# Sums of squares from a second, token-major load of x, and an earlier fetch of the output weights, in one encoder layer

## The chip, the cores and the metric

The kernel runs on one core of a Trainium2 chip, in float32. The measure is device time in microseconds of one execution, lower is better. A core has five engines that run their own instruction streams and wait for each other by semaphores: PE (TensorE, the matmuls; its loading of weights is listed apart as PEld), DVE (VectorE), ACT (ScalarE), POOL (GpSimd) and SP (SyncE, which here only issues transfers). Matmul results land in PSUM, everything else lives in SBUF.

## What is computed

One layer of an encoder on 1024 tokens of width 1024. The parts that matter here:

```python
h = rms_norm(x, norm1_g)                 # x * rsqrt(mean(x*x over the width) + eps) * gain
proj = h @ w_in                          # q, k, v (512 wide each) and u (512 wide)
a = neighbourhood_attention(rms_norm(q), rms_norm(k), v, rpb)   # 8 heads x 64
p = multiscale_pool(u, w_pool, pool_scale)
x = x + concat(a, p) @ w_out             # the output projection and its residual
h2 = rms_norm(x, norm2_g)
x = x + (silu(h2 @ w_gate) * (h2 @ w_up)) @ w_down
```

## The kernel before

Every operand of a matmul is split into a high part and a low part (`split`: ACT casts, DVE subtracts), and each product is three matmuls: high by high, high by low, low by high. `x` lies in HBM in two layouts. `xT` has the width on the 128 partitions, in 8 chunks `k` of 128x1024; `xt` has the tokens on the partitions, in 8 tiles `t` of 128x1024. All loads go through `fetch` (line 120), which takes one of 45 equal SBUF buffers and issues the transfer on SP's queue. SP works off its row in order, with at most eight transfers under way.

**Start.** SP fetches `xT` chunk by chunk, with the first weights `w1` in between, then `wp` and the first `wu` (the weights of the pooling branch). For each chunk `cook_x_` (line 170) lets ACT write `xh`, the high part of gain times `x`, DVE write `xl`, the low part, ACT write the squares `xsq`, and POOL add these up in `acc`; the last addition is shared by POOL and DVE. The first projection runs over `k`, and for each `k` over the token tiles `t` (8 for the first two chunks, 6 for the others), into PSUM banks `pj`. Its matmuls do not wait for the norm: `1/rms` comes in later, when a bank is read. At `k == KSS == 6` sixteen matmul instructions with a column of ones turn `acc` into the sums per token in a corner of a `pj` bank (`ss_ps`); from it come `vx`, `evx` and `rstd` (`rsqrt`: a logarithm and an exponential on ACT, then three Newton steps on DVE). After the last chunk TensorE does 18 matmuls for tile 6, then the first transposes `qkt` (`turn(0)`). These read `qn`, the normalised q and k that `pair(0)` makes on ACT and DVE once `rstd` is there.

**Middle.** Attention goes in steps named by head pair, column block and row block (2_3_1 is pair 2, block 3, row block 1). One step's scores `s` are transposed two steps later (`pt`), and multiplied with the values three steps later (`po`); in between lie the exponential on ACT, a scaling on POOL, and `split` into `pt_h` (ACT) and `pt_l` (DVE). Between the steps a generator, `g_dense` (line 802), feeds TensorE with dense work: projections, then the output projection `w_out` in two column halves. The output weights `wo_c_h` (chunk pair `c`, half `h`) come through `fetch_wo` and are split by `cook_wo`. At pair 3, `proj_shift` sends eight transfers on SP's queue that shift the values across partitions (`vsh`, `vsl`).

**End.** The last products of the down projection add into four quarters `c` of the output. `down` fills a PSUM bank, `dadd` adds it to the result on DVE, and `ship` sends it out.

A scheduler sets the order of most instructions before the program runs; those marked by `keep`, `keepd` and `pin` stay in the order in which they are written. On each engine the order is then fixed, and an instruction that waits holds up all behind it.

Of the kernel before, what the change touches and what calls it, by code (L numbers as in the profile page):

```python
# [54 lines left out]
def hybrid_block(ctx, tc, xT, xt, w1, wu, rpbx, wpool, wout, wgu, wd, g2, sm, out):  # L55
# [112 lines left out]
    acc = None  # L168

    def cook_x_(k):  # L170
        nonlocal acc
        raw = raws.pop(("x", k))
        h = slot(F32R, f"xh_{k}")
        l = slot(F32R, f"xl_{k}")
        n = 512 if k == 0 else T
        for c in range(0, T, n):
            cs = slice(c, c + n)
            keep(nc.scalar.activation(h[:, cs], raw[:, cs], AF.Copy, scale=g1_sb[:, k : k + 1]))  # L178
            nc.vector.scalar_tensor_tensor(  # L179
                out=l[:, cs],  # L180
                in0=raw[:, cs],
                scalar=g1_sb[:, k : k + 1],
                in1=h[:, cs].bitcast(F32),
                op0=ALU.mult,
                op1=ALU.subtract,
            )
            yield
        sq = slot(F32, f"xsq_{k}")
        nc.scalar.activation(sq, raw, AF.Square)
        if k:  # L190
            m = 512 if k == KC - 1 else 0
            nc.gpsimd.tensor_tensor(out=acc[:, m:], in0=acc[:, m:], in1=sq[:, m:], op=ALU.add)
            if m:
                nc.vector.tensor_tensor(out=acc[:, :m], in0=acc[:, :m], in1=sq[:, :m], op=ALU.add)
        else:
            acc = sq
        xh.append(h)
        xl.append(l)
# [267 lines left out]
    for i in range(4):  # L466
        if i:
            fetch_w1(0, i)
            fetch(("x", 2 * i), xT[2 * i], [P, T])
        fetch(("x", 2 * i + 1), xT[2 * i + 1], [P, T])  # L470
        if i == 3:
            fetch(("wp",), wpool, [P, 4, P])
    fetch_wu(0)
    pin_act = True
    for i in range(4):
# [8 lines left out]
        cook_x(2 * i + 1)  # L484
    pin_act = False
    one1 = up.tile([P, 1], F32, name="one1", bufs=1)
    nc.gpsimd.memset(one1, 1.0)
# [5 lines left out]
    ss_ps = pj[0][:, 384 : 384 + NT]  # L493
    for k in range(KC):
        ts = range(8 if k < KE else 6)
        for h in ((0, 1, 2),) if k > 1 else ((0, 1), (2,)) if k else ((0,), (1,), (2,)):
            for t in ts:
                if k == KSS:
                    for s in (t,) if t < 4 else (2 * t - 4, 2 * t - 3):
                        mm(  # L500
                            ss_ps[:, s : s + 1],
                            acc[:, s * P : s * P + P],
                            one1,
                            start=False,
                            stop=True,
                            skip_group_check=True,
                        )
                for i in h:
                    proj_pass(0, t, pj[t], k, i)
        if k == KSS:  # L510
            nc.vector.tensor_scalar(
                out=vx, in0=ss_ps, scalar1=1.0 / DM, scalar2=EPS, op0=ALU.mult, op1=ALU.add
# [289 lines left out]
    def g_dense():  # L802
# [4 lines left out]
        x2.extend(slot(F32, f"x2_{t}") for t in range(NT))  # L807
        for t in range(4):
            nc.sync.dma_start(out=x2[t], in_=xt[t])
        yield "wo"  # L810
        gs = [w_out(t, 0, six, 0) for t in range(3)]
# [6 lines left out]
        for c2 in (2, 3):  # L818
            fetch_wo(c2, 1)
# [8 lines left out]
        for t in range(4):  # L828
            for i, _ in enumerate(w_out(t, 1, six, 0)):
                if i % 3 == 2 and t < 3:  # L830
                    split_mix(six[2 * t + i // 3], 1, nc.scalar, (nc.gpsimd, nc.vector)[i // 3])
                yield
            nc.sync.dma_start(out=x2[4 + t], in_=xt[4 + t])
# [457 lines left out]
    for n in range(len(works)):  # L1291
# [5 lines left out]
        if not chain:  # L1297
            banks = [bank(pool[c], f"p{'aabccdd'[k]}_{g}_{c}") for c in range(4)]
        for c in range(4):
            ps = banks[c]  # L1300
            step_ = 256 if last and k == 6 and c == 3 else 512
            for n0 in range(0, 512, step_):
                n1 = n0 + step_
                down(g, ps[:, n0:n1], c, o, bo, chain, n0, n1)
# [86 lines left out]
```

## Time and profile before

| | |
|---|---|
| three timed runs | 1032.41 us median (1028.47 to 1033.79) |
| profiled execution | 1032.75 us, of which the span of instructions 1031.0 us |
| PE busy | 1010.6 us, 98% of the span |
| DVE / ACT / POOL busy | 64% / 41% / 41% |
| chain that ended last | PE 91%, DVE 4%, issue 2%, ACT 2%, DMA 1% |
| HBM | 86.25 MB read, 28.57 MB written |

PE counts as busy while a matmul is in the array, at full or at half clock. The time that PE could give back is therefore in two places: where it is idle, and where its granted clock (1.0 is 2.4 GHz) is below one. Both are found by stage, in the busy time by stretches, and then instruction by instruction in the timeline. In the timeline the bracket at the end of a row is the idle time of the engine in front of the instruction and what ended it.

### The profile page before, as it was taken

What the parts mean: (1) busy time and instruction counts of PE and PEld (TensorE: products, weight loads), DVE (VectorE), ACT (ScalarE), POOL (GpSimd) and SP (SyncE); (2) the same over time, 40 slices, a digit from 0 to 9 for tenths busy, and PEclk for the clock granted to TensorE, in tenths of its full rate; (3) what the DMA queues carried; (4) which work ended last, traced back from release to release, by engine and by line L of the source; (5) the groups of instructions that cost most, each with busy time, mean ns of one, the idle gap of its engine ahead of it and who ended that gap; (6) DMA issues with size and microseconds to landing.
All of it is one profiled execution on the core that took longest, in us unless ns stands there. A gap on an engine that the chain in (4) does not pass through costs nothing.

```text
span 1031.0 us, 13679 instructions
## 1 busy us (share of the span) xinstructions
PE 1010.6 (98%) x4909; PEld 869.1 (84%) x4909; DVE 662.5 (64%) x1115; ACT 426.8 (41%) x868; POOL 419.9 (41%) x456
## 2 busy tenths in 40 slices
PE   8899999999899998999999999999999999999998
PEld 7888999999788887888888888888888888888887
DVE  7767766667663568765655455455552499988872
ACT  8233566666762336522332333333231354533410
POOL 7210324244461146376559558558644400000170
PEclk9999999999999999999999999999999999999999
DMA  8100513143620323114233233233126984373402
GB/s 296 55 29 1 126 49 108 35 125 109 201 80 22 124 101 113 52 63 143 110 125 113 72 122 113 72 123 113 72 82 214 345 275 153 107 243 121 125 31 93
DMA packets 48821, 119.93 MB, mean 116 GB/s; under 512 B 5168, under 2 KB 13872, under 8 KB 48752
## 3 DMA queue, kind: packets, MB, share of 16 engines
q1 hardware_dynamic: 41824, 94.65, 28.2%
q0 software_dynamic: 5632, 20.19, 5.2%
q10 hardware_dynamic: 1296, 4.20, 1.0%
q8 instruction: 39, 0.64, 0.3%
q14 instruction: 30, 0.25, 0.1%
HBM read 86.25 MB, written 28.57 MB: 111 GB/s over the span
## 4 chain that ended last, share of the span: by engine, by line
PE 91%; DVE 4%; issue 2%; ACT 2%; DMA 1%; SPq 0%; ACTq 0%; DVEq 0%
PE w L89 12%; PE z L89 12%; PE pj L89 11%; PE x L89 11%; PE pw L89 7%; PE pd L89 6%; PE y L89 6%; PE pc L89 6%; PE pa L89 6%; PE pu L89 4%; PE pb L89 3%; PE s L89 2%; PE po L89 2%; PE pt L94 1%; DVE xl L179 1%
## 5 line engine op out<-in xcount | busy, mean ns | idle before, releaser
L89 PE MATMUL x<-b_h,w 128*128 128x512 f32 x352 | 115.8, 391 | 0.0
L89 PE MATMUL pw<-wo,mx 128*128 128x512 f32 x384 | 94.4, 397 | 0.5 <-DVE vnl L291 0.3
L89 PE MATMUL pj<-w1h,xl 128*128 128x384 f32 x256 | 85.0, 341 | 4.3 <-DVE xl L179 4.3
L89 PE MATMUL pj<-w1h,xh 128*128 128x384 f32 x256 | 88.4, 349 | 0.4 <-ACT xh L178 0.4
L89 PE MATMUL pj<-w1l,xh 128*128 128x384 f32 x256 | 86.0, 340 | 0.0
L1317 POOL TENSOR_TENSOR x2r<-x2r,u 128x512 f32<-128x512 f32 x12 | 23.8, 2020 | 149.8 <-DVE u L1277 149.8
L89 PEld LDWEIGHTS pw<-wo,mx 128*128 128x128 f32 x384 | 70.9, 189 | 14.8 <-DVE vnl L291 0.7
L89 PEld LDWEIGHTS x<-b_h,w 128*128 128x128 f32 x352 | 66.0, 188 | 13.6
L615 POOL TENSOR_SCALAR e<-e,r 128x256 f32<-128x256 f32 (+1 forms) x64 | 36.9, 577 | 82.2 <-DVE r L614 81.9
L1038 POOL TENSOR_TENSOR ur<-ur,gr 128x512 f32<-128x512 f32 x33 | 52.9, 1604 | 40.2 <-issue 22.0
L89 PE MATMUL x<-b_l,w 128*128 128x512 f32 x176 | 68.6, 390 | 0.0
L116 DVE TENSOR_TENSOR w_s<-sa,w_s 128x512 fp32r<-128x512 f32 x44 | 45.3, 1029 | 25.4 <-ACT w_s L115 25.4
L115 ACT CAST a_h<-raw_a 128x1024 fp32r<-128x1024 f32 (+1 forms) x42 | 41.0, 978 | 49.5 <-PE pc L89 13.8
L89 PE MATMUL z<-bt_h,w_s 128*128 128x512 f32 x176 | 57.9, 389 | 0.0
L89 PE MATMUL y<-bt_h,w_s 128*128 128x512 f32 x176 | 57.8, 390 | 0.0
L89 PE MATMUL z<-bt_h,w 128*128 128x512 f32 x176 | 57.7, 389 | 0.0
L89 PE MATMUL w<-b_h,w_s 128*128 128x512 f32 x176 | 57.7, 389 | 0.0
L89 PE MATMUL w<-bt_h,w_s 128*128 128x512 f32 x176 | 57.7, 389 | 0.0
L571 POOL TENSOR_TENSOR qbdl<-qf,qbdh 64x128 fp32r<-64x128 f32 x64 | 31.5, 492 | 56.3 <-ACT qbdh L570 44.3
L89 PEld LDWEIGHTS pj<-w1h,xl 128*128 128x128 f32 x256 | 48.8, 192 | 5.2 <-DVE xl L179 5.2
L991 POOL TENSOR_TENSOR sa<-raw_g,raw_g 128x512 f32<-128x512 f32 x11 | 14.7, 1338 | 94.2 <-DMA raw_g<-in_wgu 87.1
L116 DVE TENSOR_TENSOR a_l<-raw_a,a_h 128x1024 fp32r<-128x1024 f32 (+1 forms) x42 | 49.8, 1189 | 3.4 <-ACT a_h L115 3.1
(247 smaller groups left out, 2820.4 us busy)
## 6 DMA issues: line engine op xcount, KB each, us to landing
raw_a<-gsd SPq DMA_DIRECT2D x77, 256.0 KB, 3.8
raw_g<-in_wgu SPq DMA_DIRECT2D x22, 512.0 KB, 3.8
raw_u<-in_wgu SPq DMA_DIRECT2D x22, 512.0 KB, 3.8
gsd<-gr POOLq DMA_DIRECT2D x22, 512.0 KB, 4.0
raw_d<-in_wd SPq DMA_DIRECT2D x20, 512.0 KB, 4.4
raw_w<-in_w SPq DMA_DIRECT2D x15, 384.0 KB, 3.8
gsd<-ur POOLq DMA_DIRECT2D x11, 512.0 KB, 3.3
nb<-in_rpbx SPq DMA_DIRECT2D x12, 448.0 KB, 3.5
```

What stands on the lines that cost most here:

```text
L89: i = nc.tensor.matmul(*a, **k)
L94: i = nc.tensor.transpose(*a)
L115: keep(nc.scalar.copy(h, src))
L116: keepd(nc.vector.tensor_tensor(out=l, in0=src, in1=h.bitcast(F32), op=ALU.subtract))
L179: nc.vector.scalar_tensor_tensor(out=l[:, cs], in0=raw[:, cs], scalar=g1_sb[:, k : k + 1], in1=h[:, cs].bitcast(F32), op0=ALU.mult, op1=AL ...
L571: nc.gpsimd.tensor_tensor(out=bl[pr, qs, j, :], in0=qv[pr, qs, b, :], in1=bh[pr, qs, j, :].bitcast(F32), op=ALU.subtract,)
L615: nc.gpsimd.tensor_scalar(out=e[:, :n], in0=e[:, :n], scalar1=r, scalar2=1.0, op0=ALU.mult, op1=ALU.mult)
L991: tt(out=s1, in0=r0[:, 1], in1=r1[:, 1], op=ALU.add)
L1038: eng.tensor_tensor(out=res[i][c][:, l], in0=src, in1=g, op=ALU.mult)
L1317: nc.gpsimd.tensor_tensor(out=q, in0=q, in1=U2[c], op=ALU.add)
```

## The change

Squares: instead of squaring the chunks of `xT` and adding them on POOL, the kernel fetches all eight tiles of `xt` behind `xT`, and ACT squares each with a sum over its row, which gives the sum per token in a column of `ssx`. `acc`, the column of ones and its matmuls are gone; `wp` is fetched behind the first `wu`. Output weights: the fetch of `wo_2_1` and `wo_3_1` moves up, directly behind the first four residual tiles; the buffers of the other four residual tiles are taken one by one, where each is fetched. End: in the last group, the last quarter of the last two products is done in two halves, with the second half in a PSUM bank of its own.

```diff
 def cook_x_(k):
     ...
-        sq = slot(F32, f"xsq_{k}")
-        nc.scalar.activation(sq, raw, AF.Square)
-        if k:
-            m = 512 if k == KC - 1 else 0
-            nc.gpsimd.tensor_tensor(out=acc[:, m:], in0=acc[:, m:], in1=sq[:, m:], op=ALU.add)
-            if m:
-                nc.vector.tensor_tensor(out=acc[:, :m], in0=acc[:, :m], in1=sq[:, :m], op=ALU.add)
-        else:
-            acc = sq
...
         fetch(("x", 2 * i + 1), xT[2 * i + 1], [P, T])
-        if i == 3:
-            fetch(("wp",), wpool, [P, 4, P])
+    for t in range(NT):
+        fetch(("xt", t), xt[t], None)
     fetch_wu(0)
+    fetch(("wp",), wpool, [P, 4, P])
...
         cook_x(2 * i + 1)
+    ssx = cp.tile([P, NT], F32, name="ssx")
+    for t in range(NT):
+        raw = raws.pop(("xt", t))
+        keep(nc.scalar.activation(raw, raw, AF.Square, accum_out=ssx[:, t : t + 1]))
     pin_act = False
-    one1 = up.tile([P, 1], F32, name="one1", bufs=1)
-    nc.gpsimd.memset(one1, 1.0)
...
-                if k == KSS:
-                    for s in (t,) if t < 4 else (2 * t - 4, 2 * t - 3):
-                        mm(
-                            ss_ps[:, s : s + 1],
-                            acc[:, s * P : s * P + P],
-                            one1,
...
-                out=vx, in0=ss_ps, scalar1=1.0 / DM, scalar2=EPS, op0=ALU.mult, op1=ALU.add
+                out=vx, in0=ssx, scalar1=1.0 / DM, scalar2=EPS, op0=ALU.mult, op1=ALU.add
...
-        x2.extend(slot(F32, f"x2_{t}") for t in range(NT))
+        x2.extend(slot(F32, f"x2_{t}") for t in range(4))
         for t in range(4):
             nc.sync.dma_start(out=x2[t], in_=xt[t])
         yield "wo"
+        for c2 in (2, 3):
+            fetch_wo(c2, 1)
...
         for g in gs:
             next(g, None)
-        for c2 in (2, 3):
-            fetch_wo(c2, 1)
         yield from w_out(3, 0, six, 0)
...
+            x2.append(slot(F32, f"x2_{4 + t}"))
             nc.sync.dma_start(out=x2[4 + t], in_=xt[4 + t])
...
+        if last and k == 5:
+            spare = bank(A[0], "pd_end")
         for c in range(4):
-            ps = banks[c]
-            step_ = 256 if last and k == 6 and c == 3 else 512
+            step_ = 256 if last and k > 4 and c == 3 else 512
             for n0 in range(0, 512, step_):
                 n1 = n0 + step_
+                ps = spare if n0 else banks[c]
```

How the rows of instructions stand, at the three places where the order decides. In the names, a number such as `raw_wo_2_1_3548` ends with the number of the buffer.

ACT at the start, before: the last chunk, its square, the weights of the pooling branch, then the two steps of `rstd` and the first read of a `pj` bank.

```order
L178 ACTIVATE xh_7_220<-raw_x_7_146,sm_sb_77 128x1024
L189 ACTIVATE xsq_7_224<-raw_x_7_146 128x1024
L115 CAST wuh_0_242<-raw_wu_0_150 128x1024
L115 CAST wp_hl_591<-raw_wp_148 128x512
L100 ACTIVATE rsq_x_402<-vx_84 128x8
L101 ACTIVATE rstd_86<-rsq_x_402 128x8
L248 ACTIVATE sq_0_0_429<-pj_0_0_246 128x256
```

ACT at the start, now, from the last chunk on (the squares of tiles 1 to 6 are left out):

```order
L175 ACTIVATE xh_7_216<-raw_x_7_146,sm_sb_77 128x1024
L477 ACTIVATE raw_xt_0_148,ssx_220<-raw_xt_0_148 128x1024
...
L477 ACTIVATE raw_xt_7_162,ssx_220<-raw_xt_7_162 128x1024
L115 CAST wuh_0_241<-raw_wu_0_164 128x1024
L100 ACTIVATE rsq_x_393<-vx_84 128x8
L115 CAST wp_hl_582<-raw_wp_166 128x512
L101 ACTIVATE rstd_86<-rsq_x_393 128x8
L236 ACTIVATE sq_0_0_420<-pj_0_0_245 128x256
```

The eight squares stand together behind all chunks, and the cast of `wu` stands between them and the steps of `rstd`.

SP in the middle, before: the fourth residual tile, a bias tile, the eight shifts (six left out), then the output weights.

```order
L809 DMA x2_3_3225<-in_xt 128x1024
L560 DMA nb_3_0_3264<-in_rpbx 128x896
L324 DMA vsh_3_3367<-vnh_3_2438 96x4x128
...
L327 DMA vsl_3_3368<-vnl_3_2439 96x4x128
L123 DMA raw_wo_2_1_3548<-in_wout 128x1024
L123 DMA raw_wo_3_1_3550<-in_wout 128x1024
L560 DMA nb_3_1_3405<-in_rpbx 128x896
L123 DMA raw_wo_0_1_3629<-in_wout 128x1024
```

SP in the middle, now:

```order
L789 DMA x2_3_3216<-in_xt 128x1024
L123 DMA raw_wo_2_1_3243<-in_wout 128x1024
L123 DMA raw_wo_3_1_3245<-in_wout 128x1024
L540 DMA nb_3_0_3255<-in_rpbx 128x896
L312 DMA vsh_3_3358<-vnh_3_2429 96x4x128
...
L315 DMA vsl_3_3359<-vnl_3_2430 96x4x128
L123 DMA raw_wo_0_1_3616<-in_wout 128x1024
L540 DMA nb_3_1_3396<-in_rpbx 128x896
```

Two weight loads moved ahead of the shifts, and `raw_wo_0_1` now follows the last shift.

ACT in the middle, before, from the exponential of step 2_3_1 to that of 3_0_0 (five rows in between are left out):

```order
L612 ACTIVATE e_2_3_1_3271,sm_2_3_1_3274<-e_2_3_1_3271,m_2_3_1_3272 128x384
L316 ACTIVATE qf_3_2435<-qkt_3_3_3294,qscale_78 128x256
...
L115 CAST pt_h_1131<-pt_2_3_1_3353 128x3x128
L612 ACTIVATE e_2_3_3_3345,sm_2_3_3_3348<-e_2_3_3_3345,m_2_3_3_3346 128x256
L115 CAST wo_2_1_0_3623<-raw_wo_2_1_3548 128x512 x2
L115 CAST pt_h_1131<-pt_2_3_2_3389 128x3x128
L612 ACTIVATE e_3_0_0_3381,sm_3_0_0_3384<-e_3_0_0_3381,m_3_0_0_3382 128x256
```

ACT in the middle, now, the same stretch:

```order
L592 ACTIVATE e_2_3_1_3262,sm_2_3_1_3265<-e_2_3_1_3262,m_2_3_1_3263 128x384
L115 CAST wo_2_1_0_3610<-raw_wo_2_1_3243 128x512 x2
...
L592 ACTIVATE e_2_3_2_3305,sm_2_3_2_3308<-e_2_3_2_3305,m_2_3_2_3306 128x384
L115 CAST wo_3_1_0_3618<-raw_wo_3_1_3245 128x512 x2
L550 CAST qbdh1_94<-qf_3_2426 64x2x64 x2
L115 CAST pt_h_1122<-pt_2_3_1_3344 128x3x128
L592 ACTIVATE e_2_3_3_3336,sm_2_3_3_3339<-e_2_3_3_3336,m_2_3_3_3337 128x256
L115 CAST wo_0_1_0_3624<-raw_wo_0_1_3616 128x512 x2
L115 CAST pt_h_1122<-pt_2_3_2_3380 128x3x128
```

The cast of `wo_2_1` moved up behind step 2_3_1, that of `wo_3_1` behind 2_3_2, and that of `wo_0_1`, which stood behind step 3_0_1, now stands behind 2_3_3.

## Rows read from the trace of the kernel before

**Rows 1.** Busy time by stretches, start; us, busy us (count) per engine, PEclk, DMA, GB/s.

```profile
17.50:22.30 4.80, 4.80 (x19) 4.80 (x20) 4.80 (x2) 4.80 (x6) 4.72 (x2) 0.65 0.98 355
27.25:33.64 6.39, 6.38 (x34) 5.81 (x34) 6.39 (x4) 0.00 (x0) 4.43 (x7) 1.00 0.24 69
35.54:39.46 3.92, 3.92 (x15) 3.92 (x16) 1.69 (x2) 0.00 (x0) 0.00 (x0) 0.56 0.16 63
```

**Rows 2.** Timeline of PE, start; start us, us, engine, line, operation, out<-in, [idle before].

```profile
14.28 0.33 PE L89 MATMUL pj<-w1h,xh 128*128 128x384 f32 x1
...
17.50 0.44 PE L89 MATMUL pj<-w1h,xl 128*128 128x384 f32 x1 [2.71 <-DVE xl L179]
...
27.25 0.45 PE L89 MATMUL pj<-w1h,xl 128*128 128x384 f32 x1 [1.63 <-DVE xl L179]
...
35.54 0.38 PE L89 MATMUL pj<-one,xsq 128*128 128x1 f32 x2 [1.90 <-DVE xsq L194]
...
42.14 0.34 PE L89 MATMUL pj<-w1h,xh 128*128 128x384 f32 x1
...
45.30 0.33 PE L89 MATMUL pj<-w1h,xh 128*128 128x384 f32 x1
...
48.41 0.60 PE L94 MATMUL qkt<-ident,qn 128*128 128x128 f32 x4
```

**Rows 3.** Timeline of DVE and of POOL, start.

```profile
9.78 1.28 DVE L179 SCALAR_TENSOR_TENSOR xl<-raw_x,sm_sb,xh 128x1024 fp32r<-128x1024 f32 x1 [2.04 <-ACT xh L178]
...
23.78 6.76 DVE L179 SCALAR_TENSOR_TENSOR xl<-raw_x,sm_sb,xh 128x1024 fp32r<-128x1024 f32 x2
...
32.42 2.47 DVE L179 SCALAR_TENSOR_TENSOR xl<-raw_x,sm_sb,xh 128x1024 fp32r<-128x1024 f32 x2
...
13.56 15.89 POOL L192 TENSOR_TENSOR xsq<-xsq,xsq 128x1024 f32<-128x1024 f32 x5 [0.24 <-ACT xsq L189]
```

**Rows 4.** DMA view of the first 50 us, GB/s in 40 slices of 1.25 us.

```profile
GB/s 0 91 346 222 322 329 402 419 415 404 419 419 406 405 406 405 259 338 95 0 0 0 80 241 0 0 72 315 334 12 0 0 0 0 0 0 0 7 0 0
```

**Rows 5.** Timeline of ACT and of DVE, first projection and first normalisation.

```profile
8.59 1.15 ACT L178 ACTIVATE xh<-raw_x,sm_sb 128x1024 fp32r<-128x1024 f32 x1 [0.58 <-DMA raw_x<-in_xT]
...
24.73 1.03 ACT L115 CAST wuh<-raw_wu 128x1024 fp32r<-128x1024 f32 x1
...
35.41 1.21 DVE L116 TENSOR_TENSOR wul<-raw_wu,wuh 128x1024 fp32r<-128x1024 f32 x1
36.55 0.68 DVE L116 TENSOR_TENSOR wp_hl<-raw_wp,wp_hl 128x512 fp32r<-128x512 f32 x1
...
42.40 0.17 DVE L102 TENSOR_TENSOR rsq_x<-rstd 128x8 f32<-128x8 f32 x1 [0.31 <-ACT rstd L101]
...
46.14 0.76 DVE L275 TENSOR_TENSOR qn<-pj,y 128x256 f32<-128x256 f32 x2
```

**Rows 6.** Chain that ended last, second norm; start us, us, what (square with sum).

```profile
375.43 1.16 ACT junk L935 x2
```

**Rows 7.** Timeline of PE, ACT and SP in the middle.

```profile
276.71 0.45 PE L89 MATMUL po<-pt_h,vnh 128*128 128x384 f32 x1 [1.92 <-ACT pt_h L115]
277.61 0.44 PE L89 MATMUL po<-pt_l,vnh 128*128 128x384 f32 x1 [0.45 <-DVE pt_l L116]
...
288.81 0.39 PE L89 MATMUL po<-pt_l,vnh 128*128 128x256 f32 x1 [1.54 <-DVE pt_l L116]
...
275.14 1.14 ACT L115 CAST wo<-raw_wo 128x512 fp32r<-128x512 f32 x2 [3.58 <-DMA raw_wo<-in_wout]
...
269.59 0.62 SPq L327 DMA_DIRECT2D vsl<-vnl  x1
270.25 1.11 SPq L123 DMA_DIRECT2D raw_wo<-in_wout  x2
```

**Rows 8.** Busy time by stretches, middle.

```profile
278.00:282.30 4.30, 4.30 (x17) 3.68 (x16) 3.79 (x10) 3.12 (x10) 3.90 (x5) 0.60 0.77 267
```

**Rows 9.** Timeline of PE, second half of the last quarter.

```profile
1026.01 0.38 PE L89 MATMUL pd<-db_h,a_h 128*128 128x256 f32 x1 [0.59 <-DVE x2r L1277]
```

More of the change, by code (lines that the diff above doesn't have):

```diff
@@ L166, in cook_w1 @@
             pass
-    acc = None
     def cook_x_(k):
-        nonlocal acc
         raw = raws.pop(("x", k))
@@ L492, in hybrid_block @@
     pin = True
-    ss_ps = pj[0][:, 384 : 384 + NT]
     for k in range(KC):
@@ L497, in hybrid_block @@
             for t in ts:
-                if k == KSS:
-                    for s in (t,) if t < 4 else (2 * t - 4, 2 * t - 3):
-                        mm(
-                            ss_ps[:, s : s + 1],
-                            acc[:, s * P : s * P + P],
-                            one1,
[L504 to L507, printed above, removed]
                 for i in h:
```

## The prediction

> **What bounds the kernel now.** I read the page first: TensorE is busy in 98% of the span and carries 91% of the chain that ended last, so a change pays only where TensorE stands still, runs at its lower clock, or is given less to do. The busy time by stage shows such places at the start, around 275 us and at the very end. Then I read those places instruction by instruction.
>
> At the start TensorE waits three times in the first projection: 2.71 us for `xl` of chunk 2, 1.63 us for `xl` of a later chunk, 1.90 us for the sum of squares `xsq` [rows 2]. After the first and the last of these waits the granted clock is 0.65 and 0.56 over four to five microseconds, most of them at 1.2 GHz instead of 2.4 [rows 1]. `xl` is late because VectorE is slow while POOL adds squares: the same 128x1024 instruction takes 1.28 us before POOL starts, about 3.4 us (6.76 for two, from 23.78) beside POOL's five additions that run from 13.56 for 15.89 us, and about 1.2 us (2.47 for two) after POOL has finished [rows 3]. Around 275 us ScalarE stands 3.58 us in front of the cast of an output weight that SP issued at 270.25, behind the eight transfers that shift the values; TensorE then waits 1.92 and 0.45 us, runs at clock 0.60 for 4.3 us, and waits again for 1.54 us at 288.81 [rows 7, 8].
>
> **The change part by part. Start, what is removed.** Eight squares leave ScalarE's row in front of the casts of `x`, seven additions leave POOL, half an addition leaves VectorE, 16 one-column matmuls leave TensorE. VectorE then needs for two chunks two `xl` of 1.28 us and one `w1l` of at most 1.21 us (the row of a wider one, 128x1024, [rows 5]): 3.8 us. TensorE needs 36 matmuls for two chunks, and the 18 of the last chunk, from 42.14 to 45.30, take 3.16 us at full clock [rows 2], so 6.3 us. VectorE stays ahead, and so do the loads: 17.5 us suffice for all of `x` and the weights (below), while the last chunk is used from 30 us. So TensorE runs through. It is at 14.28 us at chunk 2, as before [rows 2]; six chunks of 3.16 us end at 33.2 instead of 45.30. That is **12.1 us** less, with waits, slow clock and one-column matmuls in it. The first transposes follow 3.11 us behind that end, 48.41 before [rows 2], so TensorE wants them at 36.3.
>
> **Start, what is added.** Eight tiles of `x` in the other layout, 4.19 MB, come behind `x` on SP's queue, and the weights `wu` and `wp` of the pooling branch behind these. ScalarE squares each tile with a sum per row; the kernel's own second norm does the same at 1.16 us a tile [rows 6]. Then `vx` and `rstd` follow, and only then the normalisation that the transposes wait for. The transfer rate sets this: the slices add up to 5.75 MB (all of `x` and the first weights) at 17.5 us, and the later full slices read 402 to 419 GB/s [rows 4]. At 410 the eight tiles take 10.2 us, so their bytes are in at 27.7. A transfer is announced later than its last byte: the fifth of the queue had its 1.44 MB in by 6.9 us, yet ScalarE waited for it until 8.59 [rows 4, 5], 1.7 us more. So the last tile is there at 29.4 and its square done at 30.6. ScalarE's row puts the cast of `wu` next, whose half megabyte lands 1.3 us behind the last tile, at 30.7: done at 31.7 with its 1.03 us [rows 5]. VectorE's row has `wul` (1.21) and the low part of `wp` (0.68) in front of the Newton steps for `rstd`: 33.6. From the first such step to the end of the first normalised pair it took 42.40 to 46.90, 4.5 us [rows 5], most of it VectorE's own work. The transposes can start at 38.1, and TensorE **waits 1.8 us** where it waited for nothing. The waits of 1.90 and 2.71 us were followed by the slow clock, that of 1.63 was not [rows 1, 2]; 1.8 is nearer to 1.90, so I charge the slow clock too: 3.92 us at 0.56 and 4.80 at 0.65 each lost 1.7 us [rows 1]. Start: 12.1 - 1.8 - 1.7 = **8.6 us**. Bounds: nothing lost, 12.1; tiles at the 322 GB/s of an early slice [rows 4], 13.0 us instead of 10.2 and 0.3 more for `wu`, so 3.1 more waiting, 5.5.
>
> The slices show 402 to 419 GB/s on this one core [rows 4]. The Trainium skill ("DMA: Bandwidth & Descriptors", Specifications) puts the share of HBM of one core at about 358 GB/s, which speaks against loading `x` twice; the trace does not bear that figure out here. By it the tiles would take 11.7 us instead of 10.2, and the time below would be 1.7 us higher.
>
> What costs nothing: the tiles take eight buffers where the squares took eight; `wu` is used only behind the first transposes, and its low part is ready at 32.9; `wp` is needed much later still. If the DMA queue were slow, this cover goes last, since `rstd` waits for the same queue.
>
> **Middle.** Two weight loads, `raw_wo_2_1` and `raw_wo_3_1`, go in front of the shifts, and their casts go three and two score steps ahead on ScalarE. Since that is free time there, they fit. But the order shows that the place they leave is filled: behind the last shift SP now issues `raw_wo_0_1`, and its cast stands in ScalarE's row directly behind the exponential of step 2_3_3 and in front of `pt_h` of 2_3_2, exactly where the cast of `wo_2_1` stood. In the times of before, SP is through with the shifts at 270.2 (the last starts at 269.59), and the load needs the 4.9 us from 270.25 to 275.14 again [rows 7]. Queued behind that cast are `pt_h` and, on VectorE, `pt_l`, and TensorE's value matmuls wait for both. So the 1.92 and 0.45 us and the slow clock stay. What goes: later ScalarE and VectorE hold two casts less, and `pt_l` is moved ahead of the score addition at the 1.54 us wait; I count 1.0 us of it. The cast of `wo_3_1` now stands in front of `pt_h` of 2_3_1: 0.2 us. Net **0.8 us**. Bounds: all three waits gone and with them 1.7 us of slow clock (4.3 us at 0.60 [rows 8]), 5.6 us; a new wait like the 1.54 one, -1.5. POOL's `nb_3_1` and an addition for `mx` now stand in front of the scaling of step 3_0_0; that is inside the lower bound. The residual loads 4 to 7 get buffers later, but their sums come last in the output projection, which covers them. In the second norm some transposes and casts swap places; zero, with plus or minus the 1.54 as bounds.
>
> **End.** The second half of the last quarter goes into a bank of its own, and the 0.59 us in which TensorE waited for the sum of the first half [rows 9] goes. Twelve more, narrower matmuls cost a little: **0.45 us**, between 0 and 0.59.
>
> **Sum.** 8.6 + 0.8 + 0.45 = 9.85 us. The profiled execution took 1032.75 us, span 1031.0 with 1.75 around it; the median of the three timed runs is 0.3 lower, the runs span 1028.5 to 1033.8. 1032.75 - 9.85 = **1022.9 us**.
>
> **Rivals.** First, `rstd` is in time (tiles land 1.8 us sooner than I count): 12.1 + 0.8 + 0.45, **1019.4 us**. For it: the lag of 1.7 us is read from one transfer. Against: three steps of two other tensors stand in front of `rstd`.
>
> Second, the middle wait really goes, because `raw_wo_0_1` lands earlier than its forerunner or ScalarE reaches it later: 8.6 + 5.6 + 0.45, **1018.1 us**. Against it: same place in both queues.
>
> Third, POOL was not what slowed VectorE (it might be the loads): `xl` stays as late as now, and only the wait for `xsq` and the work behind it go: chunk 6 starts at 33.6, where chunk 5 ends, and chunk 7 ends at 40.0 instead of 45.30: 5.3 + 0.8 + 0.45, **1026.2 us**. Against it: the two `xl` from 23.78 were slow although the slices read zero there (23.75 to 27.5 us, [rows 4]), and fast as soon as POOL had stopped [rows 3].
>
> Fourth, the tiles are slow and the middle gets a new wait: 5.5 - 1.5, **1028.8 us**, no change that can be told.
>
> Fifth, slower: the second copy of `x` comes so slowly that `rstd` stalls everything. Place: the first transposes. Each microsecond of delay beyond the 38.1 costs one. The whole gain of 9.85 is gone when they come that much later, so from a last tile at 39.3, which is 209 GB/s for the tiles (20.1 us for 4.19 MB); at 160 GB/s, 26.2 us, the result is **1039 us**. Against it: with eight transfers under way the slices read 322 and more [rows 4].
>
> **How the numbers follow.** Forecast 50%, first rival 20%, second 12%, third 6%, fourth 9%, fifth 3%. What these runs can tell from no change is about 0.5%, 5.2 us: faster means below 1027.2. Faster: 0.88; same 0.09; slower 0.03. The range leaves out the fourth and fifth and a little at the low end, where first and second come together (1014.6): **1016 to 1027 us**.
>
> **What would show it.** In the profile after: `xl` at about 1.25 us each, no wait of TensorE between 10 and 33 us, the last chunk's end near 33.2, the last square near 30.6, and a wait of about 1.8 us before the first transposes. In the middle ScalarE waits some 3 us for `raw_wo`, still just ahead of `pt_h`. At the end no gap between the two halves. I am wrong if `xl` stays at 2 us or more, if the last square ends after 33 us, or if ScalarE does not stand before a `wo` cast around 260 to 266 us.

## The result, and the profile after

The changed kernel takes 1024.41 us (median of 6 runs, 1023.47 to 1024.95); the kernel before, beside it on the same chip, 1033.1 us. The ratio is 0.9919, with a 95% interval of 0.9894 to 0.9944. The profiled execution took 1024.31 us, its span 1022.4, so 8.4 us less than the profiled execution of before. The forecast was 1022.9 (1016 to 1027).

The page after; busy time and share of the span per engine, then HBM traffic, then the chain that ended last.

```profile
PE 1007.9 (99%) x4905; PEld 866.5 (85%) x4905; DVE 648.6 (63%) x1115; ACT 429.5 (42%) x876; POOL 400.5 (39%) x448
...
HBM read 90.45 MB, written 28.57 MB: 116 GB/s over the span
...
PE 93%; DVE 4%; ACT 1%; issue 1%; DMA 1%; POOL 0%; ACTq 0%; DVEq 0%; SPq 0%; POOLq 0%
```

TensorE was busy for 1010.6 us and is for 1007.9. The other 6 us of the gain are idle time that has gone. Four megabytes more are read.

**Start.** Timeline of VectorE, then of ScalarE, then of TensorE after (start us, us, engine, line, operation, out<-in, [idle before]), which answer to [rows 2, 3, 5]:

```profile
18.89 2.65 DVE L176 SCALAR_TENSOR_TENSOR xl<-raw_x,sm_sb,xh 128x1024 fp32r<-128x1024 f32 x2
...
32.32 1.23 DVE L116 TENSOR_TENSOR wul<-raw_wu,wuh 128x1024 fp32r<-128x1024 f32 x1 [0.86 <-PE pj L89]
...
34.07 0.16 DVE L102 TENSOR_TENSOR rsq_x<-rstd 128x8 f32<-128x8 f32 x1
...
37.91 0.75 DVE L263 TENSOR_TENSOR qn<-pj,y 128x256 f32<-128x256 f32 x2
...
40.96 0.75 DVE L263 TENSOR_TENSOR qn<-pj,y 128x256 f32<-128x256 f32 x2
```

```profile
29.90 1.06 ACT L477 ACTIVATE raw_xt<-raw_xt 128x1024 f32<-128x1024 f32 x1
30.86 0.18 ACT L477 ACTIVATION_READ_ACCUMULATOR raw_xt<-raw_xt 128x1 f32 x1
```

```profile
36.12 0.34 PE L89 MATMUL pj<-w1h,xl 128*128 128x384 f32 x1
38.48 0.79 PE L94 MATMUL qkt<-ident,qn 128*128 128x128 f32 x4 [2.02 <-ACT vnh L277]
...
41.53 0.30 PE L94 MATMUL qkt<-ident,qn 128*128 128x128 f32 x1 [0.66 <-ACT sq L236]
41.59 0.48 PE L89 MATMUL pu<-xh,wuh 128*128 128x512 f32 x1
```

`xl` takes 1.3 us each (2.65 for two) up to the last. The waits of TensorE for `xl` and `xsq` are gone. New are 2.02 us in front of the first transposes and 0.66 in front of the second. Both stand behind the normalisation that follows `rstd`; the square that the second row names is ScalarE's work for the next pair, and it ends while VectorE makes the second pair of `qn` (40.96 to 41.71). The last square of `x` starts as its tile lands: the eight tiles are issued from 10.6 to 19.0 us and take 9.6 to 10.9 us to land, so the last lands at 29.9 at the latest.

Busy time by stretches after, which answers to [rows 1]: us, busy us (count) of PE, PEld, DVE, ACT and POOL, PEclk, DMA, GB/s. The wait, and what follows it up to the first `pu`:

```profile
36.46:38.48 2.02, 0.00 (x0) 0.03 (x1) 1.88 (x9) 1.48 (x6) 0.00 (x0) 1.00 0.04 16
38.48:41.59 3.11, 2.45 (x15) 2.03 (x15) 2.93 (x12) 1.68 (x7) 0.00 (x0) 1.00 0.16 13
```

The clock stays full behind a wait that the prediction had charged with 1.7 us of slow clock.

DMA view of the first 50 us after, GB/s in slices of 1.25 us, beside [rows 4]:

```profile
GB/s 0 79 335 250 311 374 395 398 396 414 418 410 420 419 416 410 403 406 410 403 413 419 401 388 421 402 407 391 172 29 7 0 0 179 148 0 0 0 0 0
```

**Middle.** Timeline of ScalarE and TensorE after, and then the busy time of the stretch behind the waits, which answer to [rows 7, 8]:

```profile
265.77 1.14 ACT L115 CAST wo<-raw_wo 128x512 fp32r<-128x512 f32 x2 [2.22 <-DMA raw_wo<-in_wout]
...
267.35 0.44 PE L89 MATMUL po<-pt_h,vnh 128*128 128x384 f32 x1 [0.47 <-ACT pt_h L115]
268.98 0.44 PE L89 MATMUL po<-pt_l,vnh 128*128 128x384 f32 x1 [1.19 <-DVE pt_l L116]
...
278.88 0.39 PE L89 MATMUL po<-pt_l,vnh 128*128 128x256 f32 x1 [0.44 <-DVE pt_l L116]
```

```profile
269.43:274.00 4.57, 4.57 (x18) 3.95 (x18) 3.13 (x10) 3.77 (x10) 4.40 (x6) 0.63 0.37 126
```

ScalarE stands before a `wo` cast in the same place, one load later in the row, and the slow clock follows as before (0.63 here, 0.60 in [rows 8]).

**Second norm.** The same waits stand in both profiles, but not the same clock behind them. Timeline of TensorE and busy time by stretches: first two fences of before, then two of after.

```profile
403.73 0.63 PE L94 MATMUL ht_t<-ident,x 128*128 128x128 f32 x4 [1.55 <-DVE bt_l L116]
...
405.76 0.66 PE L94 MATMUL ht_t<-ident,x 128*128 128x128 f32 x4
406.17 0.48 PE L89 MATMUL x<-b_h,w 128*128 128x512 f32 x1
```

```profile
405.76:409.26 3.50, 3.50 (x19) 2.96 (x20) 3.10 (x5) 1.80 (x5) 3.50 (x3) 1.00 0.23 25
```

```profile
394.50 0.63 PE L94 MATMUL ht_t<-ident,x 128*128 128x128 f32 x4 [1.56 <-DVE bt_l L116]
...
396.54 1.11 PE L94 MATMUL ht_t<-ident,x 128*128 128x128 f32 x4
```

```profile
396.60:400.10 3.50, 3.50 (x15) 2.96 (x15) 3.29 (x5) 2.78 (x6) 3.42 (x4) 0.58 0.29 64
```

Four transposes that took 0.66 us take 1.11, at a clock of 0.58.

**End.** Timeline of TensorE after, which answers to [rows 9]; the second half follows without a gap.

```profile
1017.52 0.28 PE L89 MATMUL pd<-db_h,a_l 128*128 128x256 f32 x1
1017.64 0.28 PE L89 MATMUL pd_end<-db_h,a_h 128*128 128x256 f32 x1
```

The instructions at the borders of the stages stand in all kernels of this study, so their start times divide each profile in the same way. The table gives the start of the first `pu`, and the time from there to the transposes `qkt` of pair 3, on to the first `ht` (second norm), on to the first `ht_t` that reads `t`, on to the first `pa` (down projection), and on to the last matmul. All are from the timelines of TensorE, in us. In one profile a stage can hold a spell of slow clock, some microseconds at a granted clock of 0.50 to 0.71, and in another profile of the same kernel none.

| kernel | first pu | to qkt | to ht | to ht_t | to pa | to the end |
|---|---|---|---|---|---|---|
| before | 50.45 | 209.18 | 94.08 | 34.03 | 429.38 | 210.30 |
| before, again | 51.62 | 209.18 | 93.34 | 34.03 | 430.76 | 210.31 |
| after | 41.59 | 209.35 | 93.55 | 34.05 | 430.77 | 209.65 |
| after, again | 42.23 | 209.59 | 93.81 | 34.05 | 430.03 | 209.65 |
| start_only | 42.57 | 210.21 | 94.82 | 34.04 | 430.26 | 210.31 |
| wo_only | 48.33 | 209.18 | 94.28 | 34.03 | 430.74 | 210.32 |
| no_pool_adds | 39.89 | 209.18 | 92.46 | 34.03 | 429.40 | 210.31 |
| pool_back | 46.06 | 209.56 | 92.55 | 34.05 | 430.75 | 209.65 |
| more_bytes | 45.14 | 210.38 | 92.26 | 34.05 | 429.37 | 209.65 |
| rstd_first0 | 41.12 | 209.57 | 92.71 | 34.05 | 430.01 | 209.65 |
| wu_on_pool | 41.25 | 209.28 | 92.58 | 34.04 | 430.01 | 209.65 |
| wo3_early | 41.46 | 211.21 | 92.54 | 34.04 | 429.36 | 209.66 |
| wu_in_gap | 38.82 | 210.46 | 93.92 | 34.04 | 430.42 | 209.65 |

From before to after: start 8.86 less, to `qkt` 0.17 more, to `ht` 0.53 less, to `ht_t` 0.02 more, to `pa` 1.39 more (in the second norm; about half of it is slow clock, see the last experiment), end 0.65 less. That is 8.46 us up to the last matmul.

### The profile page after: what moved, and what is told of

Same layout as the page of the kernel before. It is cut to its first block, busy times and chain, and to the rows that moved or that the text cites. A ratio compares the mean times of both kernels' runs of the same rounds, so it can differ in the third digit from the quotient of the medians.

```text
span 1022.4 us, 13679 instructions
## 1 busy us (share of the span) xinstructions
PE 1007.9 (99%) x4905; PEld 866.5 (85%) x4905; DVE 648.6 (63%) x1115; ACT 429.5 (42%) x876; POOL 400.5 (39%) x448
## 4 chain that ended last, share of the span: by engine, by line
PE 93%; DVE 4%; ACT 1%; issue 1%; DMA 1%; POOL 0%; ACTq 0%; DVEq 0%; SPq 0%; POOLq 0%
PE pj L89 12%; PE z L89 12%; PE w L89 12%; PE x L89 11%; PE pw L89 7%; PE pc L89 6%; PE pa L89 6%; PE y L89 6%; PE pd L89 6%; PE pu L89 4%; PE pb L89 3%; PE po L89 3%; PE s L89 3%; PE pt L94 2%; PE qkt L94 1%
## 5 line engine op out<-in xcount | busy, mean ns | idle before, releaser
L595 POOL TENSOR_SCALAR e<-e,r 128x256 f32<-128x256 f32 (+1 forms) x64 | 39.5, 618 | 75.8 <-DVE r L594 75.1
L1019 POOL TENSOR_TENSOR ur<-ur,gr 128x512 f32<-128x512 f32 x33 | 52.8, 1601 | 39.7 <-issue 22.0
L116 DVE TENSOR_TENSOR w_s<-sa,w_s 128x512 fp32r<-128x512 f32 x44 | 45.5, 1034 | 27.8 <-ACT w_s L115 27.7
L581 DVE CUSTOM_DVE_ANT_0 e<-s,nb 128x256 f32<-128x256 f32 (+1 forms) x64 | 31.1, 486 | 33.7 <-PE s L89 32.9
```

Of the source, the lines that this page charges most:

```text
L116: keepd(nc.vector.tensor_tensor(out=l, in0=src, in1=h.bitcast(F32), op=ALU.subtract))
L581: nc.vector.tensor_tensor_reduce(out=e[:, :n], in0=ps[:, :n], in1=nb[:, BCOL[Q] : BCOL[Q] + n], scale=1.0, scalar=BIG, op0=ALU.add, op1=AL ...
L595: nc.gpsimd.tensor_scalar(out=e[:, :n], in0=e[:, :n], scalar1=r, scalar2=1.0, op0=ALU.mult, op1=ALU.mult)
L1019: eng.tensor_tensor(out=res[i][c][:, l], in0=src, in1=g, op=ALU.mult)
```

## The experiments

**The start alone, and the output weights alone.** Each undoes the other parts of the change.

```diff
 # start_only: the changed kernel with
-        x2.extend(slot(F32, f"x2_{t}") for t in range(4))
+        x2.extend(slot(F32, f"x2_{t}") for t in range(NT))
...
         yield "wo"
-        for c2 in (2, 3):
-            fetch_wo(c2, 1)
...
         for g in gs:
             next(g, None)
+        for c2 in (2, 3):
+            fetch_wo(c2, 1)
...
-            step_ = 256 if last and k > 4 and c == 3 else 512
+            step_ = 256 if last and k == 6 and c == 3 else 512
```

> The kernel before with the start of the change alone (squares by ScalarE from the second copy of x, no POOL additions); output weights and end as before. Theory (the start carries the gain, by POOL leaving VectorE alone): first pu at about 41.6 us instead of 50.45, so 8.9 us less than before, about 1024.2 us; the waits in the middle come back at about 1.9 + 0.45 and 1.5 us, so about 0.3 to 1 us slower than the whole change. Rival (the middle or the end carries a good part): over 1026 us. The clock after the waits of the second norm: full, if the earlier output weights made it slow in the whole change (then 1.4 us less, 1022.8); slow, if it comes from the start.

Measured: 1023.44 us, ratio 0.9934 (0.9911 to 0.9957). That agrees with the changed kernel's 0.9919: the start carries the gain. The profile is of the slowest of its seven executions, 1027.49 us. In it the first `pu` comes at 42.57, later than the 41.6 expected, because TensorE waits 2.95 us for `qn` and runs at 0.57 from the transposes up to there. The slow clock of the second norm is there too, so the earlier weights don't cause it.

```diff
 # wo_only: the kernel before with
-        x2.extend(slot(F32, f"x2_{t}") for t in range(NT))
+        x2.extend(slot(F32, f"x2_{t}") for t in range(4))
...
         yield "wo"
+        for c2 in (2, 3):
+            fetch_wo(c2, 1)
...
+            x2.append(slot(F32, f"x2_{4 + t}"))
```

> The kernel before with the earlier fetch of the output weights alone. Theory (another weight, raw_wo_0_1, takes the place behind the shifts): ScalarE still stands 2 to 3.6 us in front of a cast of wo right ahead of pt_h of the same step, TensorE waits 0.5 to 1.9 and 0.5 to 1.2 us there, and the slow clock follows; 0.3 to 0.8 us less than before, ratio 0.9993 or so. Rival (the wait really goes): 5.6 us less, about 1027.5, and full clock around 275 to 285 us.

Measured: 1032.45 us, ratio 1.0007 (0.9989 to 1.0025). Timeline of ScalarE in wo_only:

```profile
272.85 1.14 ACT L115 CAST wo<-raw_wo 128x512 fp32r<-128x512 f32 x2 [2.74 <-DMA raw_wo<-in_wout]
```

The wait is where the order had put it. The rival of 5.6 us falls, and not even the small gain can be told from nothing.

**POOL taken away, and POOL put back.** The first leaves all additions out of the kernel before, so its sums of squares are those of the last chunk alone. The second adds seven additions to the changed kernel that nothing needs.

```diff
 # no_pool_adds: the kernel before with
         nc.scalar.activation(sq, raw, AF.Square)
-        if k:
-            m = 512 if k == KC - 1 else 0
-            nc.gpsimd.tensor_tensor(out=acc[:, m:], in0=acc[:, m:], in1=sq[:, m:], op=ALU.add)
-            if m:
-                nc.vector.tensor_tensor(out=acc[:, :m], in0=acc[:, :m], in1=sq[:, :m], op=ALU.add)
-        else:
-            acc = sq
+        acc = sq
 # pool_back: the changed kernel with
+        if k:
+            nc.gpsimd.tensor_tensor(out=side, in0=raw, in1=h.bitcast(F32), op=ALU.add)
         xh.append(h)
```

> The kernel before without its seven additions on POOL and the half addition on VectorE: the squares stay, but the sums of squares are those of the last chunk alone. Theory (POOL slows VectorE): the 128x1024 subtraction xl takes 1.28 us throughout, TensorE does not wait from 10 to 33 us, its first transposes come at about 36.4 instead of 48.41, no wait for rstd: 12 us less, about 1021 us. Rival (the loads slow VectorE): xl stays at 2 to 3.4 us from 14 to 30 us, the waits of 2.71 and 1.63 stay, and at most 5.3 us go: 1027.8 us.

> The changed kernel with seven additions 128x1024 on POOL beside the chunks (x plus its high part, into a buffer that nothing reads). Theory (POOL slows VectorE): xl takes about 3.4 us beside them, TensorE waits again for xl, 2 to 5 us in all with some slow clock, the first transposes come 2 to 5 us later than 38.48, and the time is 2 to 5 us above the changed kernel's 1024.4. Rival (POOL was not the cause): xl stays at 1.28 us and the time at 1024.4.

Measured: without the additions 1020.81 us, ratio 0.9898 (0.9864 to 0.9932); with additions put back 1028.12 us, ratio 0.9955 (0.9938 to 0.9973). Timeline of VectorE and TensorE in no_pool_adds, then of POOL, VectorE and TensorE in pool_back:

```profile
23.03 1.28 DVE L179 SCALAR_TENSOR_TENSOR xl<-raw_x,sm_sb,xh 128x1024 fp32r<-128x1024 f32 x1 [0.70 <-ACT xh L178]
...
37.85 0.60 PE L94 MATMUL qkt<-ident,qn 128*128 128x128 f32 x4
```

```profile
9.89 16.26 POOL L186 TENSOR_TENSOR side<-raw_x,xh 128x1024 f32<-128x1024 f32 x5 [5.58 <-ACT xh L175]
...
26.29 6.54 POOL L186 TENSOR_TENSOR side<-raw_x,xh 128x1024 f32<-128x1024 f32 x2
...
23.84 6.74 DVE L176 SCALAR_TENSOR_TENSOR xl<-raw_x,sm_sb,xh 128x1024 fp32r<-128x1024 f32 x2
...
33.57 2.47 DVE L176 SCALAR_TENSOR_TENSOR xl<-raw_x,sm_sb,xh 128x1024 fp32r<-128x1024 f32 x2
...
17.58 0.69 PE L89 MATMUL pj<-w1h,xl 128*128 128x384 f32 x1 [2.40 <-DVE xl L176]
...
44.03 0.60 PE L94 MATMUL qkt<-ident,qn 128*128 128x128 f32 x4
```

In no_pool_adds, with the loads and the squares on ScalarE as before, `xl` is fast without POOL. In pool_back it is 3.37 us with POOL instead of 1.28, and fast again once POOL has stopped. This settles the third rival: POOL was the cause. The Trainium skill ("SBUF — State Buffer", Who interferes with whom) calls the port pair that the two engines share an exclusive lock, held for a whole instruction, when VectorE's instruction has two inputs in SBUF and POOL's reads SBUF. By that rule one addition and one subtraction alternate, and 3.25 us per addition beside 3.37 per subtraction agrees.

Both times lie in the expected range, both first transposes do not. In no_pool_adds they come 1.4 us later than the 36.4 expected, without a wait; the matmuls with the column of ones are still in this kernel. In pool_back they come at 44.03, 5.5 us behind the changed kernel's, where 2 to 5 were expected; by then `rstd` is in time, so the wait of 2.02 us is gone and the first `pu` comes only 4.5 us later. The projection, which ended at 36.46, ends 7.6 us later. So about 7.6 of the 11.95 us that went at the start are POOL's brake on VectorE. The rest is argued, not tried: the kernel before also has the wait for the sum `xsq` (1.90), the slow clock behind it and the matmuls with the column of ones [rows 1, 2], and pool_back has none of them.

**More bytes ahead of the squares.**

```diff
     for t in range(NT):
+        if t < 2:
+            side = up.tile([P, T], F32, name=f"side_{t}", bufs=1)
+            nc.sync.dma_start(out=side, in_=xt[7 - t])
         fetch(("xt", t), xt[t], None)
```

> The changed kernel with two more tiles, 1.05 MB, on SP's queue ahead of the tiles that are squared (into buffers that nothing reads). Theory (the bytes ahead of the last tile set rstd, and rstd the first transposes): 2.56 us more at 410 GB/s, last square at about 33.5 instead of 30.9, first transposes at about 41.0 instead of 38.48, wait in front of them about 4.6 instead of 2.02; 2.5 us above the changed kernel, 1.7 more where the slow clock follows: 1027 to 1028.6. Rival (rstd has slack, the wait is for something else): 1024.4.

Measured: 1027.01 us, ratio 0.9952 (0.9932 to 0.9972). Timeline of ScalarE and TensorE, and the busy time of the stretch from the transposes to the first `pu`, in more_bytes:

```profile
32.65 1.06 ACT L480 ACTIVATE raw_xt<-raw_xt 128x1024 f32<-128x1024 f32 x1
...
41.25 1.14 PE L94 MATMUL qkt<-ident,qn 128*128 128x128 f32 x4 [5.17 <-DVE qn L263]
```

```profile
41.25:45.14 3.89, 3.89 (x15) 3.71 (x15) 3.71 (x14) 2.12 (x8) 0.00 (x0) 0.50 0.00 0
```

The last square starts 2.75 us later than in the first profile of the changed kernel (2.10 later than in the second, where it starts at 30.55), and the transposes follow by 2.77. Here the slow clock comes, 0.50 over 3.89 us. The bytes ahead of `rstd` cost what was expected. That the median is at the low end of 1027 to 1028.6 in spite of the slow clock is no merit of the sum: in the profile two later stages are faster than in the changed kernel's (to `ht` 92.26, to `pa` 429.37).

**`rstd` ahead of `wu` and `wp`.** Two ways, then a third that learns from both.

```diff
 # rstd_first0: the changed kernel with
-    pin_act = False
     fetch_wu(1)
     proj_alloc(0)
-    cook_wu(0)
...
+            pin_act = pin_dve = True
             rsqrt(tq, rstd, vx, NT, "x")
...
     pair(0)
+    cook_wu(0)
     pair(1)
...
     cook(("wp",), *wps)
+    pin_act = pin_dve = False
 # wu_on_pool: the same, but instead of cook_wu(0)
+    nc.gpsimd.tensor_copy(wus[0][0], raw)
+    nc.gpsimd.tensor_tensor(out=wus[0][1], in0=raw, in1=wus[0][0].bitcast(F32), op=ALU.subtract)
```

> The changed kernel with the steps of rstd directly behind the last square; the casts and subtractions of wu stand behind the first normalised pair, those of wp behind the last. Theory (1.05 us of wuh on ScalarE and 1.9 us of wul and the low part of wp on VectorE hold rstd up): rstd is done at about 32.4 instead of 34.6, first transposes at 36.5 instead of 38.48 without a wait; the second pair then waits for wul, about 1 us; first pu at about 40.6 instead of 41.59, 1 us below the changed kernel: 1023.4. Rival (the transfers or the pair itself set it): first transposes stay at 38 or later, 1024.4 or more.

> The changed kernel with the steps of rstd directly behind the last square and the high and low part of wu made by POOL alone, which is idle there. Theory (as for rstd_first0, and nothing takes the place): first transposes at 36.5, second wait under 0.7, first pu at 38.5 to 39.6 if VectorE is undisturbed, 2 to 3 us below the changed kernel, 1021.4 to 1022.4. Rival (POOL slows VectorE's short instructions as it slows the long ones): the chain from rstd to the transposes takes over 5 us instead of 3.9, first pu at 41 or later, 1024 or more.

Measured: rstd_first0 1022.89 us, ratio 0.9906 (0.9872 to 0.9939); wu_on_pool 1023.8 us, ratio 0.9911 (0.9882 to 0.9941). In rstd_first0 the transposes come at 36.75 with a wait of 0.67, although the last square started at 30.46, 0.56 later than in the first profile: the theory holds for the first transposes. The second wait is 2.0 us, twice what was expected, since `wuh` (1.03) and `wul` (1.22) stand in front of the second pair; so little is left, first `pu` at 41.12. Neither kernel can be told from the changed one (0.9919) by its time.

In wu_on_pool the transposes come at 38.07, behind a wait of 2.13 us. Timeline of VectorE and POOL there:

```profile
31.12 0.61 DVE L102 TENSOR_TENSOR rsq_x<-rstd 128x8 f32<-128x8 f32 x1 [0.31 <-ACT rstd L101]
...
31.97 2.25 DVE L104 SCALAR_TENSOR_TENSOR rstd<-rsq_x,rstd 128x8 f32<-128x8 f32 x1
...
30.67 1.04 POOL L482 CAST wuh<-raw_wu 128x1024 fp32r<-128x1024 f32 x1 [15.28 <-DVE vx L493]
31.80 2.39 POOL L483 TENSOR_TENSOR wul<-raw_wu,wuh 128x1024 fp32r<-128x1024 f32 x1
```

The last Newton step, 128x8, which takes 0.17 us elsewhere, takes 2.25 and ends as POOL's subtraction ends. So the rival holds, in a sharper form: not the pair was slow, but one short instruction stood behind one long instruction of POOL.

```diff
 # wu_in_gap: rstd_first0, but instead of cook_wu(0)
     def vals(p, tt, pss):
         proj_vals(p, tt, pss)
+        if tt == 0:
+            keep(nc.scalar.copy(wus[0][0], raw_wu))
...
     pair(1)
+    keepd(nc.vector.tensor_tensor(out=wus[0][1], in0=raw_wu, in1=wus[0][0].bitcast(F32), op=ALU.subtract))
+    dg0 = make_dg(0)
```

(`dg` is the identity scaled with `rstd`, 0.88 us on VectorE in front of the first pair in the changed kernel; a later matmul, `rb`, reads it.)

> The changed kernel with the steps of rstd directly behind the last square; the cast of wu stands in the 1.5 us in which ScalarE waited within the first normalised pair, its low part and dg behind the second pair on VectorE, wp behind the last. Theory (instructions of wu, wp and dg in front of rstd and of the pairs make both waits at the start): first transposes at 36.5 or at most 37 without a wait of over 0.5, second transposes at about 39.6 without a wait, first pu at 39.7 to 40 instead of 41.59: 1.6 to 1.9 us below the changed kernel with equal clocks elsewhere, 1022 us or a little less. Rival (the last tile's landing, which was 30.2 to 31.4 in the runs so far, sets it): first pu at 40.5 or later, within 1 us of the changed kernel.

> The changed kernel once more, beside wu_in_gap on the same chip, and a second profile of it. Theory (the slow clock after the waits of the second norm, which took 1.4 us in its first profile and none in that of before, comes and goes between executions of the same program): 1022 to 1025.5, first pu at 41 to 42 us; a spell of slow clock that stood in the first profile may be absent here, or another present. Rival (the change itself causes it by its order): slow clock from 395 to 400 us again, the same 1.4 us.

Measured on one chip: wu_in_gap 1022.22 us, ratio 0.9900 (0.9877 to 0.9923); the changed kernel 1024.96, ratio 0.9932 (0.9910 to 0.9954). The intervals overlap; the medians differ by 2.7 us, and all six runs of wu_in_gap (1020.93 to 1022.76) are faster than the fastest of the other (1023.68). Timeline of TensorE in wu_in_gap:

```profile
36.11 0.60 PE L94 MATMUL qkt<-ident,qn 128*128 128x128 f32 x4
...
38.77 0.30 PE L94 MATMUL qkt<-ident,qn 128*128 128x128 f32 x1 [0.46 <-ACT sq L236]
38.82 0.48 PE L89 MATMUL pu<-xh,wuh 128*128 128x512 f32 x1
```

The first transposes wait for nothing. The first `pu` comes 2.8 us earlier than in the first profile of the changed kernel, earlier than the 39.7 to 40 expected, though 1.1 us of that goes again up to `qkt` (210.46 instead of 209.35); 0.60 of it is a new wait at 53.81, in front of `rb`.

Timeline and busy time by stretches of the second norm in the second profile of the changed kernel:

```profile
395.66 0.63 PE L94 MATMUL ht_t<-ident,x 128*128 128x128 f32 x4 [1.55 <-DVE bt_l L116]
...
397.69 0.66 PE L94 MATMUL ht_t<-ident,x 128*128 128x128 f32 x4
398.51 0.50 PE L89 MATMUL x<-b_h,w 128*128 128x512 f32 x1 [0.16 <-ACT w L115]
```

```profile
395.00:400.00 5.00, 3.95 (x23) 2.77 (x24) 4.43 (x7) 3.23 (x7) 3.80 (x3) 1.00 0.32 105
```

The wait is the same, the clock is full, and the way to `pa` is 430.03 us instead of 430.77. So the change does not cause the slow clock, and the rival falls. The first `pu`, at 42.23, is a little later than the 41 to 42 expected.

**A third output weight ahead of the shifts.**

```diff
-        for c2 in (2, 3):
+        for c2 in (2, 3, 0):
             fetch_wo(c2, 1)
...
         cook_wo(2, 1)
-        fetch_wo(0, 1)
```

> The changed kernel with a third output weight, raw_wo_0_1, also fetched ahead of the eight shifts. Theory (the cast that waits for this load holds pt_h and pt_l up): ScalarE no longer waits for a wo there, the waits of TensorE of 0.47 and 1.19 us go, and the slow clock behind them (0.68 from 270 to 275, 1.6 us) with them: 1.7 to 3.3 us below the changed kernel, 1021.1 to 1022.7. Rival (the waits come from the length of the step's own chain, or the buffer for the third load comes late): waits of 1 us or more stay in this stretch, 1024.4.

Measured: 1023.51 us, ratio 0.9919 (0.9892 to 0.9947), the changed kernel's own; 1021.1 to 1022.7 were expected. Timeline of ScalarE and TensorE in wo3_early:

```profile
270.87 1.14 ACT L115 CAST wo<-raw_wo 128x512 fp32r<-128x512 f32 x2
...
278.74 0.38 PE L89 MATMUL po<-pt_h,vnh 128*128 128x256 f32 x1 [1.11 <-ACT pt_h L115]
...
282.64 0.44 PE L94 MATMUL pt<-ident,e 128*128 128x128 f32 x2 [0.90 <-POOL e L595]
```

No load holds ScalarE up any more, and yet TensorE waits 1.11 and 0.90 us in the stretch. So the late load is not the only cause of these waits. Full clock there proves nothing for the earlier load: four kernels that keep the late load (pool_back, more_bytes, rstd_first0, wu_on_pool) have it too, and their stage to `ht`, 92.26 to 92.71, is like the 92.54 here. Which instruction sets the pace of a score step there was not tried.

**The kernel before, once more.**

> The kernel before once more, for a second profile of it. Theory (spells come and go between executions): among the stretches 0 to 42, 275 to 285 and 395 to 410 us, at least one has another clock than in the first profile, and the span differs by about the 1.4 to 1.9 us of a spell; that would account for runs from 1028.5 to 1036.5. Rival (the clock follows from the program): the same spells in the same places, none in the second norm.

Measured: 1033.05 us (median); the profiled execution took 1034.56, its span 1032.8. Timeline and busy time by stretches of its second norm:

```profile
404.14 0.63 PE L94 MATMUL ht_t<-ident,x 128*128 128x128 f32 x4 [1.55 <-DVE bt_l L116]
```

```profile
405.00:410.00 5.00, 4.84 (x20) 3.95 (x20) 4.77 (x7) 2.99 (x6) 4.92 (x4) 0.66 0.31 83
```

The same program, the same waits, and now the slow clock: 430.76 us up to `pa` instead of 429.38. The start differs too: the first `pu` comes at 51.62 instead of 50.45. The spell comes and goes between executions. In the changed kernel it was worth 0.74 of the 1.39 us of the first comparison. The other 0.65 goes with the order in which the instructions of the second norm stand: in the changed kernel the four transposes (at 397.69 in its second profile) are followed by a wait for the weight `w`, in the kernel before `x` follows without a gap (405.76, 406.17). At full clock the three profiles with the first order take 430.0 us up to `pa` (after again, rstd_first0, wu_on_pool), the four with the second 429.4 (before, no_pool_adds, more_bytes, wo3_early).

## Why the prediction was right, step by step

Forecast 1022.9 us with a range of 1016 to 1027, measured 1024.4. The sum was 9.85 us; the last matmul came 8.46 us earlier.

**What bounds the kernel.** Right: the gain came from the start, where TensorE stood still behind VectorE, and VectorE was slow because of POOL (no_pool_adds, pool_back). One reading was loose: POOL's first addition starts at 10.78, within the `xl` of 1.28 us that is called the one before POOL; the comparison stands, since `xl` is as fast in no_pool_adds.

**Start, removed: 12.1 us.** Measured 11.95: the projection ends at 36.46 instead of 48.41.

**Start, the new wait: 1.8 us.** Measured 2.02, and 2.48 in the second profile. Each step of the chain came about half a microsecond late: last square at 29.90 (forecast 29.4), first Newton step at 34.07 (33.6), transposes at 38.48 (38.1). The mis-sized term is the lag between a tile's last byte and its landing. By the slices after, which add up to 5.77 MB at 17.5 us and read 401 to 419 GB/s from there to 28.75 us, the last tile's bytes are in at 27.7, as forecast; it lands at 29.9. That is an estimate of 2.2 us where 1.7, read from one transfer, had stood. The square itself fits: with the instruction that reads the sum out it takes 1.14 us (29.90 to 31.04) against 1.16. The cover named as costing nothing, `wu` and `wp` behind the transposes, held; that these stood in front of `rstd` was counted, and rstd_first0 shows that it was right to count it.

**Start, the slow clock: 1.7 us.** This step failed. Clock 1.00 followed the wait in both profiles of the changed kernel. What stood in its place was a term that the sum stopped short of: the second pair comes 3.05 us behind the first on VectorE (37.91 to 40.96), longer than the nine matmuls that stand between the first and the second transposes (39.02 to 40.87). So the first `pu` comes 3.11 us behind the first transposes instead of 2.04 in before. 11.95 - 2.02 - 1.07 = 8.86 against 8.6: that the sum agreed is luck, 1.7 us charged that did not come against 1.07 that came uncharged and some tenths in the other two terms. Nor is 8.86 one fixed figure: the first `pu` of the kernel before came at 50.45 and 51.62 in its two profiles, that of the changed kernel at 41.59 and 42.23.

**Middle: 0.8 us.** The order was read rightly: another load takes the place behind the shifts, and ScalarE waits 2.22 us for it (2.74 in wo_only). The size was not. Of the column "to ht", compare what had slow clock there with its like: 94.08, 93.34 and 94.82 with the old fetch, 94.28, 93.55, 93.81 and 93.92 with the new; without slow clock 92.46 with the old and 92.26 to 92.71 with the new. The term measured about 0, as the ratio of wo_only says: the wait of 1.54 us shrank to 0.44, but smaller waits came up around it. The slow clock, said to stay, came and went with either fetch.

**Second norm: zero, with 1.54 as bounds.** It lost 1.39 in the first comparison, and carried most of the 1.4 us by which the profiled execution missed the forecast. 0.74 of it is a spell of slow clock and chance: before_again has the spell, after_again does not. The other 0.65 goes with the swapped order, which the prediction saw and put at zero.

**End: 0.45 us.** Measured 0.65, in every kernel that has the edit (210.3 to 209.65). That is above the upper bound of 0.59; where the other 0.06 comes from these rows don't show.

**Rivals.** The third (POOL not the cause) and the second (the middle wait really goes) have fallen. The first, `rstd` in time, is what wu_in_gap makes true: 1019.4 were worked out for it, 1022.2 measured, since some of it is lost again before `qkt`, the 0.8 of the middle did not come, and slow clock stays in two stages of its profile. In the fourth neither condition came true. The mechanism of the fifth is real at its small end: 2.56 us more of loading moved the transposes by 2.1 to 2.8 us and the median by 2.1 to 2.6. The tiles came at 401 to 419 GB/s, so its price was never paid.

## What to carry to other kernels

An engine that looks idle is not free to use: beside POOL's additions each of VectorE's subtractions took 3.37 us instead of 1.28, and a second load of 4.19 MB was cheaper here than seven additions. Follow a new wait past the first instruction that waits: the next pair behind it had the shorter cover. Two profiles of one program differ by a spell or two of slow clock, here 0.7 to 1.4 us in a stage, so a term of that size is settled by stages in several profiles, not by one pair of spans.

## What was not expected of the hardware

A 128x8 instruction of VectorE took 2.25 us instead of 0.17 behind one subtraction of POOL, and 0.61 behind a cast of POOL (wu_on_pool). The length of a wait did not say whether slow clock follows: behind 2.02, 2.13 and 2.48 us in front of the first transposes the granted clock stayed 1.00 (after, wu_on_pool, after again), behind 2.39, 2.95 and 5.17 it fell (wo3_early 0.71 over 38 to 42 us, start_only 0.57, more_bytes 0.50), and the same waits of the second norm were followed by 1.00 in one execution and 0.66 in another. What decides it these runs don't show.
